# Runs of two, four and eight equal matrix products in the feed-forward stages of a two-layer decoder trunk

## The chip, the cores and the metric

The kernel runs on one core of one Trainium2 chip; the other cores are idle. A core has a matrix engine (TensorE, PE in the profile, with its weight loads shown apart as PEld), a vector engine (DVE), a scalar engine (ACT), a general engine (POOL) and a queue that issues the transfers (SP). The metric is the device time of one execution in microseconds (us); lower is better. The kernel before took 1003.13 us, the median of three runs that lie between 1002.96 and 1003.3 us.

## The reference, cut to what matters

Two layers, each a feed-forward sub-layer, a token-mixing sub-layer and a second feed-forward sub-layer. The input has 256 positions of 1024 features; the feed-forward width is 2816. The change touches the feed-forward sub-layers alone.

```python
def swiglu(h, w_gate_up, w_down):
    a, b = jnp.split(h @ w_gate_up, 2, axis=-1)
    return (jax.nn.silu(a) * b) @ w_down

def hybrid_layer(x, ...):
    x = x + 0.5 * swiglu(rms_norm(x, ffn1_norm), ffn1_w_gate_up, ffn1_w_down)
    ...                                    # pooling and block attention, merged by gates
    x = x + merged @ w_out
    x = x + 0.5 * swiglu(rms_norm(x, ffn2_norm), ffn2_w_gate_up, ffn2_w_down)
    return x
```

All of it is float32. With two layers there are four feed-forward stages, which are called the first to the fourth here, in the order of the program.

## The kernel before

**Numbers.** A float32 matrix is written as the sum of two parts, a high one and a low one, each of a shorter float format that TensorE multiplies quickly. A 128x128 block of weights thus has a high and a low part (`hl[h][:, 0]` and `hl[h][:, 1]`), and so has a 128x256 block of activations (`xk[:, 0]`, `xk[:, 1]`, next to each other). Three of the four partial products are formed, in two instructions. The high weights stay in the array while 512 columns stream past, both parts of the activations; then the low weights, while 256 columns stream past, the high activations alone. These two products together are called a **chain** here (`chain`, L119 to L122). Every product goes through `prod` (L117), which loads its own weights. So PE sees a long sequence of 512, 256, 512, 256, with a weight load ahead of each.

**Tiles.** Weights come in units of 1 MB, each 16 blocks (`unit`, `bring`, L72 to L95): one transfer, then a copy on ACT (high part, L102) and a subtraction on DVE (low part, L103), for each half of 8 blocks. Two units are asked for ahead.

**A feed-forward stage** (`ffn`, L262). In its first part, 22 units are multiplied with the 8 activation blocks `hk`. `pair` (L130 to L138) takes one unit: 8 steps along the features, and in each step one chain for the gate half and one for the up half, which add up in two banks of one PSUM tile (`ps[:, 0]`, `ps[:, 1]`); then ACT (L174) and DVE (L175) drain the tile. The first two units of a stage (three in the first stage) go through `two_pairs` or `pairs`, which have loops of their own. The third unit also carries two small products (`spread`, tile `st`) that sum up squares over the partitions for the norm; they stand ahead of the chain whose number is `at`. Each pair of outputs then becomes a silu, a product and another split on ACT and DVE (L302, L303, L178, L179), into the tiles `ga` (the first 16 blocks) and `gb` (the last 6).

In its second part ("down"), for each of 8 output blocks `f` there are 22 chains over `ga` and `gb` into one PSUM bank (L306 to L321). The 176 chains use 11 units, so that a unit's end and an output's end don't fall together. In the last output block of the fourth stage, `chain3` takes the place of the chain: three products of 256 columns each, so that the ends can be added up at once.

**Order.** PE's order is the order in which the program issues (`manual_schedule` for PE); ACT, DVE and the transfers are placed by a scheduler.

Of the kernel before, what the change touches and what calls it, by code (L numbers as in the profile page):

```python
# [21 lines left out]
NK = D // P  # L22
DFF = 2816
NF = DFF // P
# [11 lines left out]
C_G1, C_GM, C_G2, C_BG, C_PS, NG = 0, 8, 16, 24, 40, 44  # L36
# [3 lines left out]
def trunk_kernel(ctx: ExitStack, tc: tile.TileContext, x_in, w_in, pw_in, qkn_in, rope_in, mask_in, band_in, out):  # L40
    nc = tc.nc
# [30 lines left out]
    def unit():  # L72

        ask(2)
        return ahead.pop(0)

    def ask(n):
        while len(ahead) < n and n_unit[0] < L * LAYER:
            ahead.append(bring(n_unit[0]))
            n_unit[0] += 1  # L80
# [24 lines left out]
    def blk(hl, b, j, n=1):  # L105
        c = b * P % HALF
        return hl[b * P // HALF][:, j, c:c + n * P]


    def steps(z):  # L110

        if len(z.shape) == 3:
            z = z.rearrange("p a s -> p (a s)")
        return z.rearrange("p (s a c) -> p a s c", a=4, c=4)

    def prod(ps, w, xk, first, last):
        return mm(steps(ps), lhsT=w, rhs=steps(xk), start=first, stop=last)  # L117

    def chain(ps, hl, b, xk, first, last):  # L119

        prod(ps, blk(hl, b, 0), xk, first, False)
        return prod(ps[:, 0, :], blk(hl, b, 1), xk[:, 0, :], False, last)  # L122

    def chain3(ps, hl, b, xs, first=True, last=True):
        for i, xk in enumerate(xs):
            prod(ps, blk(hl, b + i, 0), xk[:, 0, :], first and i == 0, False)
            prod(ps, blk(hl, b + i, 0), xk[:, 1, :], False, False)
            prod(ps, blk(hl, b + i, 1), xk[:, 0, :], False, last and i == len(xs) - 1)

    def pair(hl, t, at=None, do=None):  # L130

        ps = pmm.tile([P, 2, 2, S], F32, name="ps", tag="mm")
        for k in range(NK):
            for j in range(2):
                if 2 * k + j == at:
                    do()
                chain(ps[:, j], hl, 2 * k + j, hk[k], k == 0, k == NK - 1)
        return drain(t, ps)  # L138

    def ends():  # L140
# [32 lines left out]
    def drain(t, ps):  # L173
        a = act(t, ps[:, :, 1, :], AF.Copy)  # L174
        return a.ins, tt(t, ps[:, :, 0, :], t, op=OP.add).ins  # L175

    def halves(d, v):
        act(d[:, 0, :], v, AF.Copy)  # L178
        tt(d[:, 1, :], v, d[:, 0, :].bitcast(F32), op=OP.subtract)  # L179
# [4 lines left out]
    x = gx[:, L * NG:].rearrange("p (k s) -> p k s", s=S)  # L184
# [17 lines left out]
    hk = [hx[:, k] for k in range(NK)]  # L202
    acc = acts.tile([P, S], F32, name="acc")

    def split_x(f, l, col):
        g = gain[:, l, col + f:col + f + 1]
        act(hx[:, f, 0, :], x[:, f, :], AF.Copy, scale=g)  # L207
        stt(hx[:, f, 1, :], x[:, f, :], g, hx[:, f, 0, :].bitcast(F32), op0=OP.mult, op1=OP.subtract)  # L208

    def square_x(f):  # L210
        if f == 0:
            act(acc, x[:, f, :], AF.Square)
        else:
            sq = small.tile([P, S], F32, name="sq", tag="sq", bufs=2)
            act(sq, x[:, f, :], AF.Square)
            tt(acc, acc, sq, op=OP.add)

    def prep(f, l, col):
        split_x(f, l, col)
        square_x(f)  # L220
# [13 lines left out]
    def sums():  # L234

        ah = small.tile([P, 2, S], F32R, name="ah", tag="dr", bufs=1)
        halves(ah, acc)
        return ah

    def spread(ah, st):  # L240
        for j in range(2):
            prod(st, one_r, ah[:, j, :], j == 0, j == 1)

    def factor(st):
        r = small.tile([P, S], F32, name="r", tag="r", bufs=2)
        rsqrt(r, st, 1.0 / D)
        return r
# [10 lines left out]
    def bc2(a):  # L258
        return a.unsqueeze(1).to_broadcast([P, 2, a.shape[-1]])


    def ffn(after, at, ah=None, last=False, mid=None):  # L262
        first = ah is not None

        gs = []
        for n, m in (("ga", 16), ("gb", NF - 16)):
            g = acts.tile([P, m, 2, S], F32R, name=n, tag=n)
            gs.extend(g[:, i] for i in range(m))
        n0 = 3 if first else 2
        abs_ = []  # L270
        r = None
        for i in range(NF):
            ab = tmp.tile([P, 2, S], F32, name="ab", tag="t512", bufs=5)
            abs_.append((i, ab))
            if i < n0:
                if i == n0 - 1:
                    (pairs if first else two_pairs)([unit() for _ in abs_], [t for _, t in abs_])
                continue
            if r is None:
                st = pat.tile([P, S], F32, name="st", tag="at")  # L280
                pair(unit(), ab, at, lambda: spread(ah if first else sums(), st))
                if first:
                    ask(2)
                    with tc.issue_after(last_split[1]):
                        r = factor(st)
                else:
                    r = factor(st)
                if not last:
                    rh = small.tile([P, S], F32, name="rh", tag="rh", bufs=1)
                    act(rh, r, AF.Copy, scale=0.5)  # L290
            elif first and i == 9:

                pair(unit(), ab, NK, lambda: spread(ah, pat.tile([P, S], F32, name="st", tag="at")))
            else:
                pair(unit(), ab)
            for j, ab in abs_:
                if last:
                    tt(ab, ab, bc2(r), op=OP.mult)
                else:
                    tt(ab[:, 0, :], ab[:, 0, :], r, op=OP.mult)  # L300
                sg = small.tile([P, S], F32, name="sg", tag="sg", bufs=2)
                act(sg, ab[:, 0, :], AF.Silu)  # L302
                tt(sg, sg, ab[:, 1, :], op=OP.mult)  # L303
                halves(gs[j], sg)
            abs_ = []
        for b in range(NK * NF):  # L306
            f, k = divmod(b, NF)
            if b % 16 == 0:
                hl = unit()
            if mid and b == 32:  # L310
                mid()
            if k == 0:
                ps = pat.tile([P, 2, S], F32, name="ps", tag="at")
            two = not last or f < NK - 1
            if two:
                chain(ps, hl, b % 16, gs[k], k == 0, k == NF - 1)
            else:
                chain3(ps[:, 0, :], hl, b % 16, gs[k:k + 1], k == 0, k == NF - 1)
            if k == NF - 1:
                add_x(f, ps, 0.5, two, None if last else rh)  # L320
                after(f)  # L321

    def add_x(f, ps, c, two=True, rc=None):

        t = x[:, f, :]
        if two:
            t = small.tile([P, S], F32, name="t", tag="sg", bufs=2)
            act(t, ps[:, 1, :], AF.Copy)  # L328
        if rc is not None:
            tt(t, ps[:, 0, :], t, op=OP.add)  # L330
            tt(t, t, rc, op=OP.mult)
            tt(x[:, f, :], x[:, f, :], t, op=OP.add)
            return
        if two:
            stt(t, t, c, x[:, f, :], op0=OP.mult, op1=OP.add)
        stt(x[:, f, :], ps[:, 0, :], c, t, op0=OP.mult, op1=OP.add)  # L336
# [52 lines left out]
    def turns(l):  # L389

        if l == 0:
            with tc.issue_after(last_load[0]):
                for d, z in ((rope, rope_in), (qkn, qkn_in), (mask[:, 1], mask_in), (mask[:, 2], mask_in)):
                    nc.sync.dma_start(d, z)
        cs = []
        for j in range(2):
            c = small.tile([P, 2, 2, DH], F32, name="c", tag="turn", bufs=2)
            with tc.issue_after(last_split[1]):
                for i in range(2):
                    tt(c[:, i], rope[:, i], bc2(qkn[:, l, j, i * DH:(i + 1) * DH]), op=OP.mult)  # L400
            cs.append(c)
        return cs
# [240 lines left out]
    with tc.manual_schedule(engines={E.SP, E.Activation, E.DVE}):  # L643
# [22 lines left out]
        ah = sums()  # L666
# [3 lines left out]
    ahead.extend(w[1] for w in w3)  # L670
    for l in range(L):
        cs = []
        ffn(lambda f: prep(f, l, C_GM), NK if l else NK + 1, None if l else ah, mid=lambda: cs.extend(turns(l)))
        mix(l, lambda f: prep(f, l, C_G2), cs)
        if l + 1 < L:
            ffn(lambda f: prep(f, l + 1, C_G1), NK + 1)
        else:
            ffn(lambda f: nc.sync.dma_start(out[:, f, :], x[:, f, :]), NK + 1, last=True)


# [88 lines left out]
```

## Time and profile before

| what | before |
|---|---|
| device time, median of three runs | 1003.13 us |
| device time of the profiled execution | 1006.28 us |
| its span, from the first to the last instruction | 1004.4 us |
| PE busy in the span | 997.9 us (99%), 6170 products |
| DVE busy | 806.1 us (80%) |
| ACT busy | 636.8 us (63%) |
| mean granted TensorE clock | 0.999 |
| memory traffic over the span | 191 GB/s |

The span is divided into the work of the engines. "Busy" of PE counts the time in which at least one product is under way; products overlap, the next one starting while the one before still drains, so that a busy PE is not the same as a PE at its peak. The chain of waits is the sequence of work, followed back from the last instruction, that set the end. In it, the time of a piece with a count of products divided by that count is the real step from one product to the next.

### The profile page before, as it was taken

The page shows a single profiled execution, that of the slowest core. Times are in us where ns is not written, and L with a number is a line of the kernel's source. Part 1 is how long each engine was busy: PE and PEld are TensorE (multiplying, and loading weights), DVE is VectorE, ACT ScalarE, POOL GpSimd, SP SyncE. Part 2 cuts the span into 40 slices and gives each one's busy share as a digit, 9 for nine tenths or more (in the row PEclk, how much of TensorE's full clock was granted, in tenths as well). Part 3 has the DMA queues.
Part 4 walks back from the last instruction along what each step waited for, and adds up shares of the span by engine and source line. Part 5 has one row for each costly group of instructions (what it writes and reads, how often), then busy time and mean ns, then how long its engine had stood idle before and what let it go on. Part 6 is the DMA issues. An engine that isn't in the chain of part 4 may idle for free.

```text
span 1004.4 us, 15755 instructions
## 1 busy us (share of the span) xinstructions
PE 997.9 (99%) x6170; PEld 898.7 (89%) x6170; DVE 806.1 (80%) x1326; ACT 636.8 (63%) x1017; POOL 10.6 (1%) x35
## 2 busy tenths in 40 slices
PE   9999999999999999999999999999999999999998
PEld 8889899888899988989989899898888989899887
DVE  7887777799978987776778777778997899988752
ACT  7766655657776676665557666556676777666541
POOL 0000000002000000000000000000010000000000
PEclk9999999999999999999999999999999999999999
DMA  8765665553545655655656555554536456555640
GB/s 294 266 230 182 224 210 194 184 199 107 210 168 174 215 205 204 209 184 199 207 173 208 206 201 186 201 209 151 196 119 222 163 195 213 200 191 208 211 146 22
DMA packets 30601, 192.94 MB, mean 192 GB/s; under 512 B 3392, under 2 KB 5824, under 8 KB 8000
## 3 DMA queue, kind: packets, MB, share of 16 engines
q1 hardware_dynamic: 30240, 191.69, 55.4%
q8 instruction: 48, 0.79, 0.3%
q10 hardware_dynamic: 288, 0.26, 0.1%
q14 instruction: 25, 0.20, 0.1%
HBM read 190.89 MB, written 1.05 MB: 191 GB/s over the span
## 4 chain that ended last, share of the span: by engine, by line
PE 97%; DVE 1%; ACT 0%; DMA 0%; issue 0%; SPq 0%
PE ps L117 78%; PE pt L117 9%; PE pl L117 6%; PE pe L117 2%; PE sc L431 1%; DVE hl L103 1%; PE y L467 1%; PE pt L457 1%; PE tp L422 0%; DMA raw<-w 0%; PE yp L117 0%; ACT hl L102 0%; DVE ab L300 0%; DVE r L226 0%; PE st L117 0%
## 5 line engine op out<-in xcount | busy, mean ns | idle before, releaser
L117 PE MATMUL ps<-hx,hl 128*128 128x512 f32 (+1 forms) x3200 | 543.0, 329 | 2.0 <-ACT sg L302 1.4
L117 PEld LDWEIGHTS ps<-hx,hl 128*128 128x128 f32 x3200 | 481.7, 188 | 57.6 <-ACT sg L302 1.7
L103 DVE TENSOR_TENSOR hl<-raw,hl 128x1024 fp32r<-128x1024 f32 (+2 forms) x371 | 439.8, 1192 | 111.7 <-ACT hl L102 110.0
L102 ACT ACTIVATE hl<-raw 128x1024 fp32r<-128x1024 f32 (+2 forms) x371 | 382.7, 1034 | 144.5 <-PE ps L117 98.8
L117 PE MATMUL ps<-ga,hl 128*128 128x256 f32 (+1 forms) x1040 | 176.0, 325 | 0.0
L117 PEld LDWEIGHTS ps<-ga,hl 128*128 128x128 f32 x1040 | 154.3, 188 | 16.6
L174 ACT ACTIVATE ab<-ps 128x512 f32<-128x512 f32 x84 | 50.0, 595 | 80.4 <-PE ps L117 80.1
L175 DVE TENSOR_TENSOR ab<-ps,ab 128x512 f32<-128x512 f32 x84 | 57.7, 687 | 36.5 <-ACT ab L174 36.3
L117 PE MATMUL ps<-gb,hl 128*128 128x256 f32 (+1 forms) x390 | 69.2, 325 | 0.0
L117 PEld LDWEIGHTS ps<-gb,hl 128*128 128x128 f32 x390 | 57.9, 188 | 6.2
L302 ACT ACTIVATE sg<-ab 128x256 f32<-128x256 f32 x88 | 36.2, 417 | 26.7 <-DVE ab L300 15.4
L117 PE MATMUL pt<-ax,hl 128*128 128x256 f32 x384 | 44.5, 276 | 0.0
L117 PEld LDWEIGHTS pt<-ax,hl 128*128 128x128 f32 x384 | 44.2, 188 | 0.3 <-DVE gates L175 0.3
L117 PE MATMUL pl<-hl,hx 128*128 128x512 f32 (+1 forms) x256 | 44.4, 330 | 0.0
L117 PEld LDWEIGHTS pl<-hl,hx 128*128 128x128 f32 x256 | 38.5, 188 | 4.9
L303 DVE TENSOR_TENSOR sg<-sg,ab 128x256 f32<-128x256 f32 x88 | 36.1, 418 | 0.1
L328 ACT ACTIVATE t<-ps 128x256 f32<-128x256 f32 x39 | 14.7, 378 | 27.7 <-PE ps L117 27.7
L178 ACT ACTIVATE ga<-sg 128x256 fp32r<-128x256 f32 x64 | 25.4, 406 | 8.7 <-DVE sg L303 8.5
L207 ACT ACTIVATE hx<-gx 128x256 fp32r<-128x256 f32 x48 | 23.9, 504 | 10.8 <-DVE gx L336 5.2
L300 DVE TENSOR_TENSOR ab<-ab,r 128x256 f32<-128x256 f32 x66 | 27.3, 424 | 1.7
L179 DVE TENSOR_TENSOR ga<-sg,ga 128x256 fp32r<-128x256 f32 x64 | 26.2, 418 | 1.4 <-ACT ga L178 1.4
L208 DVE SCALAR_TENSOR_TENSOR hx<-gx,hx 128x256 fp32r<-128x256 f32 x48 | 22.7, 478 | 3.4 <-ACT hx L207 3.4
(125 smaller groups left out, 685.5 us busy)
## 6 DMA issues: line engine op xcount, KB each, us to landing
raw<-w SPq DMA_DIRECT2D x176, 1024.0 KB, 4.9
raw<-w SPq DMA_DIRECT2D x9, 256.0 KB, 5.7
raw<-w SPq DMA_DIRECT2D x2, 512.0 KB, 6.6
out_dram<-gx SPq DMA_DIRECT2D x8, 128.0 KB, 1.9
gx<-x SPq DMA_DIRECT2D x3, 256.0 KB, 5.4
raw<-w SPq DMA_DIRECT2D x4, 128.0 KB, 4.0
raw<-pw SPq DMA_DIRECT2D x2, 256.0 KB, 2.6
raw<-w ACTq DMA_DIRECT2D x2, 128.0 KB, 3.7
```

Of the source, the lines that this page charges most:

```text
L102: a = act(hi, w, AF.Copy)
L103: last_split[:] = [a.ins, tt(lo, w, hi.bitcast(F32), op=OP.subtract).ins]
L117: return mm(steps(ps), lhsT=w, rhs=steps(xk), start=first, stop=last)
L174: a = act(t, ps[:, :, 1, :], AF.Copy)
L175: return a.ins, tt(t, ps[:, :, 0, :], t, op=OP.add).ins
L178: act(d[:, 0, :], v, AF.Copy)
L179: tt(d[:, 1, :], v, d[:, 0, :].bitcast(F32), op=OP.subtract)
L207: act(hx[:, f, 0, :], x[:, f, :], AF.Copy, scale=g)
L208: stt(hx[:, f, 1, :], x[:, f, :], g, hx[:, f, 0, :].bitcast(F32), op0=OP.mult, op1=OP.subtract)
L300: tt(ab[:, 0, :], ab[:, 0, :], r, op=OP.mult)
L302: act(sg, ab[:, 0, :], AF.Silu)
L303: tt(sg, sg, ab[:, 1, :], op=OP.mult)
```

## The change

The chains of a feed-forward stage are issued in runs. A run of n chains issues first the n products of 512 columns, then the n of 256 columns. In the first stage n is 1, which is the order of before; in the second it is 2, in the third 4, in the fourth 8. Nothing else is computed, and the number of products and of weight loads stays.

```diff
-    def pair(hl, t, at=None, do=None):
+    def run(steps):
+
+        for ps, hl, b, xk, first, last in steps:
+            prod(ps, blk(hl, b, 0), xk, first, False)
+        for ps, hl, b, xk, first, last in steps:
+            prod(ps[:, 0, :], blk(hl, b, 1), xk[:, 0, :], False, last)
+
+    def pair(hl, t, at=None, do=None, n=1):
 
         ps = pmm.tile([P, 2, 2, S], F32, name="ps", tag="mm")
-        for k in range(NK):
-            for j in range(2):
-                if 2 * k + j == at:
-                    do()
-                chain(ps[:, j], hl, 2 * k + j, hk[k], k == 0, k == NK - 1)
+        for b in range(0, 2 * NK, n):
+            if at is not None and b <= at < b + n:
+                do()
+            run([(ps[:, c % 2], hl, c, hk[c // 2], c < 2, c >= 2 * NK - 2) for c in range(b, b + n)])
         return drain(t, ps)
...
+        todo = []
         for b in range(NK * NF):
...
             if two:
-                chain(ps, hl, b % 16, gs[k], k == 0, k == NF - 1)
+                todo.append((ps, hl, b % 16, gs[k], k == 0, k == NF - 1))
+                if len(todo) == group or k == NF - 1 or b % 16 == 15:
+                    run(todo)
+                    todo = []
...
-        ffn(lambda f: prep(f, l, C_GM), NK if l else NK + 1, None if l else ah, mid=lambda: cs.extend(turns(l)))
+        ffn(lambda f: prep(f, l, C_GM), NK if l else NK + 1, None if l else ah, mid=lambda: cs.extend(turns(l)),
+            group=4 if l else 1)
         mix(l, lambda f: prep(f, l, C_G2), cs)
         if l + 1 < L:
-            ffn(lambda f: prep(f, l + 1, C_G1), NK + 1)
+            ffn(lambda f: prep(f, l + 1, C_G1), NK + 1, group=2)
         else:
-            ffn(lambda f: nc.sync.dma_start(out[:, f, :], x[:, f, :]), NK + 1, last=True)
+            ffn(lambda f: nc.sync.dma_start(out[:, f, :], x[:, f, :]), NK + 1, last=True, group=8)
```

`pair` gets `n=group` from `ffn`; `two_pairs`, `pairs`, `chain3` and the whole mixing stage keep their order.

On PE, in the third unit of the second feed-forward stage, this is how the order stood before around the two products of `spread` (tile `st`). A shape 128x4x32x4 is a product of 512 columns, 128x4x16x4 one of 256; the numbers tell buffers apart, `hl_3445` and `hl_3446` being the two halves of one unit.

```order
L117 MATMUL ps_3535<-hx_105,hl_3445 128x4x32x4
L117 MATMUL ps_3535<-hx_105,hl_3445 128x4x16x4
L117 MATMUL ps_3535<-hx_105,hl_3445 128x4x32x4
L117 MATMUL ps_3535<-hx_105,hl_3445 128x4x16x4
L117 MATMUL ps_3535<-hx_105,hl_3446 128x4x32x4
L117 MATMUL ps_3535<-hx_105,hl_3446 128x4x16x4
L117 MATMUL st_3526<-ah_3554,one_r_85 128x4x16x4 x2
L117 MATMUL ps_3535<-hx_105,hl_3446 128x4x32x4
L117 MATMUL ps_3535<-hx_105,hl_3446 128x4x16x4
```

And on PE at the same place of the changed kernel:

```order
L117 MATMUL ps_3535<-hx_105,hl_3445 128x4x32x4 x2
L117 MATMUL ps_3535<-hx_105,hl_3445 128x4x16x4 x2
L117 MATMUL st_3526<-ah_3552,one_r_85 128x4x16x4 x2
L117 MATMUL ps_3535<-hx_105,hl_3446 128x4x32x4 x2
L117 MATMUL ps_3535<-hx_105,hl_3446 128x4x16x4 x2
```

Equal products now stand two and two, and the `spread` stands one chain earlier, ahead of the first block of the second half instead of its second.

On PE, where the fourth stage goes over from its first part to its second, before (the last chain of the last unit, then the first chains of "down"):

```order
L117 MATMUL ps_9375<-hx_105,hl_9319 128x4x32x4
L117 MATMUL ps_9375<-hx_105,hl_9319 128x4x16x4
L117 MATMUL ps_9424<-ga_8296,hl_9368 128x4x32x4
L117 MATMUL ps_9424<-ga_8296,hl_9368 128x4x16x4
L117 MATMUL ps_9424<-ga_8296,hl_9368 128x4x32x4
```

The same place of the changed kernel, on PE, to the start of the second output block (`ps_9482`):

```order
L117 MATMUL ps_9375<-hx_105,hl_9319 128x4x32x4 x8
L117 MATMUL ps_9375<-hx_105,hl_9319 128x4x16x4 x8
L117 MATMUL ps_9424<-ga_8296,hl_9368 128x4x32x4 x8
L117 MATMUL ps_9424<-ga_8296,hl_9368 128x4x16x4 x8
L117 MATMUL ps_9424<-ga_8296,hl_9369 128x4x32x4 x8
L117 MATMUL ps_9424<-ga_8296,hl_9369 128x4x16x4 x8
L117 MATMUL ps_9424<-gb_8297,hl_9417 128x4x32x4 x6
L117 MATMUL ps_9424<-gb_8297,hl_9417 128x4x16x4 x6
L117 MATMUL ps_9482<-ga_8296,hl_9417 128x4x32x4 x2
```

The runs are of eight, but end with a unit or an output block, so that there are also runs of six, four and two in "down". The order on ACT, DVE, POOL and SP is the same row for row as before. Over the whole program, 1025 places where a 256-column product stood behind a 512-column one now have a 512-column product there, and as many have a 256-column product behind a 256-column one: 248 of each in the second stage, 368 in the third, 409 in the fourth.

More of the change, by code (lines that the diff above doesn't have):

```diff
@@ L259, in bc2, with ffn @@
         return a.unsqueeze(1).to_broadcast([P, 2, a.shape[-1]])
-    def ffn(after, at, ah=None, last=False, mid=None):
+    def ffn(after, at, ah=None, last=False, mid=None, group=1):
         first = ah is not None
@@ L280, in ffn @@
                 st = pat.tile([P, S], F32, name="st", tag="at")
-                pair(unit(), ab, at, lambda: spread(ah if first else sums(), st))
+                pair(unit(), ab, at, lambda: spread(ah if first else sums(), st), group)
                 if first:
@@ L294, in ffn @@
             else:
-                pair(unit(), ab)
+                pair(unit(), ab, n=group)
             for j, ab in abs_:
```

## The prediction

> **What bounds the kernel.** I read the page's head first, then the chain of waits.
>
> ```profile
> span 1004.4 us, 15755 instructions
> PE 997.9 (99%) x6170; PEld 898.7 (89%) x6170; DVE 806.1 (80%) x1326; ACT 636.8 (63%) x1017; POOL 10.6 (1%) x35
> PEclk9999999999999999999999999999999999999999
> PE 97%; DVE 1%; ACT 0%; DMA 0%; issue 0%; SPq 0%
> ```
>
> PE is busy throughout, at the full granted clock in every slice, and 97% of the chain that set the end is PE. No other engine can be made to matter without first holding PE up. So the question is one of PE's own pace: the step from one product to the next. A busy share can't show that, since products overlap. The pieces of the chain of waits in order of time do: each has a length and a count.
>
> ```profile
> 342.84 162.37 PE ps L117 x974
> 518.77 162.70 PE ps L117 x976
> 838.39 162.61 PE ps L117 x996
> ```
>
> These are the second, third and fourth feed-forward stage, each from its `spread` to its end, without a gap. The first has 974 products, 487 chains: 162.37 / 487 = 0.3334 us, so **a chain takes 333.4 ns**. The second gives 162.70 / 488 = 333.4 ns again. Inside a chain I look at two narrow windows of the timeline on PE, which show what was running then and when it began.
>
> ```profile
> 400.27 0.49 PE L117 MATMUL ps<-hx,hl 128*128 128x256 f32 x2
> 400.38 0.38 PE L117 MATMUL ps<-hx,hl 128*128 128x512 f32 x1
> 400.38 0.50 PE L117 MATMUL ps<-hx,hl 128*128 128x512 f32 x2
> 400.05 0.49 PE L117 MATMUL ps<-hx,hl 128*128 128x512 f32 x2
> ```
>
> A 512-column product begins at 400.05, its 256-column partner at 400.27, the next 512 at 400.38. To the two digits shown, the 512 holds PE for 0.22 us and the 256 for 0.11 us: 333.4 in all, about 221 and 112.
>
> **What the change removes and adds.** Nothing is removed or added. 1025 times (248, 368 and 409 in stages two to four), a pair of steps "512 then 256, 256 then 512" is exchanged for "512 then 512, 256 then 256". So each exchange costs X + Y - 333.4 ns, where X is the step of a 512 that is followed by a 512, Y that of a 256 followed by a 256.
>
> Y is in the trace. The last output block of the fourth stage is made of `chain3`, 256-column products alone, with the same operands and a weight load for each.
>
> ```profile
> 993.26 5.67 PE L117 MATMUL ps<-ga,hl 128*128 128x256 f32 x48
> 998.77 2.22 PE L117 MATMUL ps<-gb,hl 128*128 128x256 f32 x18
> 780.88 22.20 PE pt L117 x192
> ```
>
> From 993.26 to 998.77 there are 48 of them: 5.51 / 48 = **Y = 114.8 ns**. The branch products of the mixing stage give 22.20 / 192 = 115.6. A check: the fourth stage's piece has 996 products, 66 of them in `chain3`; 465 x 333.4 + 66 x 114.8 ns = 162.6 us, the 162.61 of the row. So a 256 costs some 3 ns more behind its own kind than in a chain, and no more: runs of 256 columns don't run into the weight load, though a load lasts longer than the step:
>
> ```profile
> L117 PEld LDWEIGHTS ps<-hx,hl 128*128 128x128 f32 x3200 | 481.7, 188 | 57.6 <-ACT sg L302 1.7 <-ACT hl L102 0.9 <-DVE hl L103 0.2
> L117 PE MATMUL ps<-ga,hl 128*128 128x512 f32 x496 | 166.8, 382 | 0.0
> L117 PE MATMUL ps<-ga,hl 128*128 128x256 f32 x544 | 141.3, 274 | 0.0
> ```
>
> At 188 ns a load outlasts a 256's step of 114.8, so loads must overlap one another. Were they serial, the exchange would cost 1025 x (188 - 115) ns = 75 us; the 114.8 excludes that.
>
> X is nowhere in the trace: no 512 stands behind a 512. The break-even is X = 333.4 - 114.8 = **218.6 ns**. Bounds from the nearest rows:
>
> - From below: a 512-column product lasts 382 ns, a 256-column one 274, so 256 columns more take 108 ns. 512 columns then take 216 ns with nothing between products. X = 216 would give 1025 x (216 + 114.8 - 333.4) = 1025 x (-2.6) = -2.7 us.
> - From above: Y plus the 108 ns for the further columns, 114.8 + 108 = 222.8, that is 1025 x 4.2 = +4.3 us.
> - In between: the 512's step in a chain, about 221, gives +2.5 us; and if the time of a product depends on its own length and on that of its neighbour, each separately, the sum can't change at all, as every kind of product and of neighbour keeps its count. That is the 218.6.
>
> I take **X = 220**, between the last two, which are the nearest rows: 1025 x (220 + 114.8 - 333.4) = 1025 x 1.4 ns = **+1.4 us**. By stage: +0.35, +0.5 and +0.6.
>
> The Trainium skill, page "TensorE: Matmul & The Clock Gate", section "Back-to-back issue gap", gives the isolated step of a warm product as N/2.4 + 2.5 ns, 215.8 for 512 columns and 109.2 for 256; a chain would be 325.0 by it. The trace's 333.4 and 114.8 are both longer, so it doesn't hold in this stream of loads and products; if it held for the 512s in a run, the sum would be an estimated 1025 x (215.8 + 114.8 - 333.4) = -2.9 us.
>
> **What else moves.** Four edits cost nothing, each with its cover.
>
> ```profile
> 831.82 0.42 DVE L179 TENSOR_TENSOR ah<-acc,ah 128x256 fp32r<-128x256 f32 x1
> 837.99 0.39 PE L117 MATMUL st<-ah,one_r 128*128 128x256 f32 x2
> 941.92 5.49 PE L117 MATMUL ps<-ga,hl 128*128 128x512 f32 x32
> 947.02 0.42 DVE L179 TENSOR_TENSOR gb<-sg,gb 128x256 fp32r<-128x256 f32 x1
> ```
>
> - The `spread` moves one chain earlier, 0.33 us. Its input `ah` is written at 832.24 and it ran at 837.99: 5.4 us of cover remain. Without it, PE would stand, and all behind it.
> - In "down", a run needs its activations earlier. The tightest is the last block of `gb` in the fourth stage, written at 947.44. Before, its 512 began 21 chains into the stretch at 941.92 + 7.00 = 948.92; now it stands behind 16 chains and five 512s, at 941.92 + 5.33 + 1.10 = 948.35. 0.9 us of cover remain; if it were gone, PE would stand by what is missing, once, well under 1 us.
> - The last product into a PSUM tile and the last use of a half unit fall at the ends of runs, where they stood before: runs end at each output block and each unit, and 2, 4 and 8 all divide a half unit of 8 blocks in the first part. In "down", runs that don't start on a multiple of their length free a half up to 8 products later, under 2 us; the next splits go to other buffers, and PE shows no wait for a split in these stages (the pieces above are unbroken).
> - ACT, DVE, POOL and SP keep their order, and the transfers their triggers; DVE and ACT are 20% and 37% idle.
>
> A second weighing: the same page's section "Step-by-step: what each phase is for" says that loads are pulled ahead into a background buffer while a product runs, which speaks against runs of 256, as each load has only a short product to hide under. The 114.8 already holds what that costs here; by the page alone, with the 107 ns a load takes in its section "LDWEIGHTS (loading the stationary operand)", it would be an estimated 109 or so and the sum would fall by 6 us.
>
> **The rivals.**
>
> *A: slower, the rhythm is lost.* The trace has the same chains at other paces, at the same clock.
>
> ```profile
> 703.43 10.85 PE pl L117 x64
> 714.28 10.74 PE pt L117 x64
> 761.65 11.11 PE ps L117 x64
> 813.82 10.67 PE ps L117 x64
> ```
>
> 32 chains each: 339.1, 335.6, 347.2 and 333.4 ns. The third is `pair` itself, with the operands of a feed-forward stage, behind other small products (its start may hold another wait, so I don't price by it). So what a chain costs above its columns, 3 x 108 = 324, depends on how products and loads fall on one another, and 333.4 is the best that any stretch shows. Runs change that rhythm in every chain of three stages: 496 + 496 + 474 = 1466. At the 339.1 of the query and key products it costs 1466 x 5.7 = +8.4 us; at X = 222.8 without more, +4.3. It decides from X + Y over 335.4, where the loss passes 2 us. For it: a 256 behind a 256 already pays 3 ns more. Against it: the feed-forward stages hold their pace over 488 chains, whatever went before. Time: 1005.6 to 1011.5.
>
> *B: faster, switching is what costs.* A chain has 9 ns above its columns, and if most of it comes from the change of length, runs save it. Then X falls to its lower bound, 216, and the time by 2.7 us, to 1000.4. For it: nothing shows a 512 behind a 512, and a longer product hides a load best. Against it: a 256 behind a 256, with no change of length, is not cheaper but dearer.
>
> *C: no change at all,* as the counts of kinds are kept: 1003.1, inside the forecast's band. That the order isn't what it says is excluded: on PE the equal products stand in runs.
>
> **How the numbers follow.** The sum is made against the profiled execution: 1006.28 us of device time, its span of 1004.4 and 1.9 around it. 1006.28 + 1.4 is 0.14% more. The median shown is 1003.13, so the forecast is 1003.13 x 1.0014 = **1004.5 us**. A measurement here can tell about 0.2%, 2 us, from no change; in X that is 216.6 to 220.6 when Y holds. The forecast and C, inside 2 us: 0.40. A: 0.34, as the bound from above and the spread of rhythms both lie there, but the forecast's X is itself only 0.6 ns short of it. B: 0.26. The range has B's 1000.4 in it with a little of a Y below 114.8, and A's price at 339.1 lies above its middle: 999.8 to 1009.5, which leaves out the greater losses (a tenth) and the greater gains (a little less).
>
> **What would show it.** The three pieces of the chain of waits for stages two to four, 162.37, 162.70 and 162.61 us before, should read about 162.7, 163.2 and 163.2. If they fall instead, by an amount that goes with 248, 368 and 409, B is right and X is 218.6 less the fall per exchange. If they rise by 2 us and more, A is right, and the starts in a narrow window tell whether the 512s or the 256s pay. The first stage and the mixing stages must stay as they were; if they move, it is something other than the order. A gap ahead of `st` or in the first output block of "down" would show that a cover was misjudged. The forecast is wrong if X lies outside 216.6 to 220.6.

## The result, and the profile after

The changed kernel takes 1016.54 us (median of four runs, 1016.31 to 1018.21), the kernel before 1003.21 us beside it. The ratio is 1.0128, with a 95% interval from 1.0116 to 1.0141: slower by 13.3 us, outside the predicted range.

The head of the page of the changed kernel, with the same lines as shown of before:

```profile
span 1014.7 us, 15755 instructions
PE 1009.7 (100%) x6170; PEld 901.2 (89%) x6170; DVE 806.1 (79%) x1326; ACT 636.1 (63%) x1017; POOL 10.6 (1%) x35
PEclk9999999999999999999999999999999999999999
PE 99%; DMA 1%; ACT 0%; DVE 0%; issue 0%
```

Nothing waits that did not wait before: the instructions, DVE's and ACT's busy time and the clock are the same, and PE is busy for 11.8 us more. Its busy time grew with the same 6170 products, so the products follow each other more slowly. The chain of waits in order of time shows where; the pieces are the four feed-forward stages (start, length, products):

```profile
58.09 125.33 PE ps L117 x752
340.04 165.91 PE ps L117 x976
519.82 167.99 PE ps L117 x976
844.16 167.07 PE ps L117 x998
```

The first stage, with runs of one, has 376 chains in 125.33 us: 333.3 ns a chain, as before. The second has 165.91 / 488 = 340.0, the third 167.99 / 488 = 344.2, the fourth (167.07 - 66 x 0.1148) / 466 = 342.3, with its 66 `chain3` products taken off. Over 333.4 that is 3.2, 5.3 and 4.1 us, 12.6 of the 13.3. Each exchange of steps cost about 13, 14 and 10 ns, where +1.4 was forecast. (The span grew by 10.3 us only, because the first stage began 2.7 us later in the execution of before that was profiled, whose device time, too, lay 3 us above its median.)

A narrow view shows the products themselves. Groups by shape on PE, from 860 to 930 us, inside the fourth stage; behind the bar stand the time in which the group was at work and the mean length of one product in ns. First before, then after:

```profile
L117 PE MATMUL ps<-hx,hl 128*128 128x512 f32 x211 | 70.4, 382 | 0.0
L117 PE MATMUL ps<-hx,hl 128*128 128x256 f32 x211 | 57.7, 273 | 0.0
```

```profile
L117 PE MATMUL ps<-hx,hl 128*128 128x512 f32 x205 | 51.2, 389 | 0.0
L117 PE MATMUL ps<-hx,hl 128*128 128x256 f32 x206 | 27.7, 276 | 0.0
```

The record of a product is longer, 389 for 382 ns with 512 columns and 276 for 273 with 256. This does not tell a stall within a product from a wait between two: the ends of products are modelled in the profile, and a 512 of the first part is recorded as ending some 160 ns after the next product starts, before (382 and a step of 221) as after (389 and 229). So the starts are used here. From them, the steps that stood open in the prediction are X = 229.1 ns (mean of 680 in the first parts; 226.7 in the 345 of the second parts; 228.3 over all 1025) and Y = 114.7 ns in the first parts, 114.8 over all. In runs of eight of the first parts, the first 512 behind a run of 256s takes 221.6, the second 224.9, the others 228 to 234.

### The profile page after: what moved, and what is told of

Same layout as the page of the kernel before. It is cut to its first block, busy times and chain, and to the rows that moved or that the text cites. A ratio compares the mean times of both kernels' runs of the same rounds, so it can differ in the third digit from the quotient of the medians.

```text
span 1014.7 us, 15755 instructions
## 1 busy us (share of the span) xinstructions
PE 1009.7 (100%) x6170; PEld 901.2 (89%) x6170; DVE 806.1 (79%) x1326; ACT 636.1 (63%) x1017; POOL 10.6 (1%) x35
## 4 chain that ended last, share of the span: by engine, by line
PE 99%; DMA 1%; ACT 0%; DVE 0%; issue 0%
PE ps L117 79%; PE pt L117 9%; PE pl L117 6%; PE pe L117 2%; DMA raw<-w 1%; PE sc L441 1%; PE y L477 1%; PE pt L467 1%; PE tp L432 0%; PE yp L117 0%; PE st L117 0%; ACT L654 0%; DVE hl L103 0%; ACT hl L102 0%; DVE gx L346 0%
## 5 line engine op out<-in xcount | busy, mean ns | idle before, releaser
L117 PE MATMUL ps<-hx,hl 128*128 128x512 f32 (+1 forms) x3200 | 551.5, 332 | 0.4 <-ACT hl L102 0.2
L117 PE MATMUL ps<-ga,hl 128*128 128x512 f32 (+1 forms) x1040 | 180.2, 328 | 0.0
L117 PEld LDWEIGHTS ps<-ga,hl 128*128 128x128 f32 x1040 | 156.9, 188 | 18.4
L117 PE MATMUL ps<-gb,hl 128*128 128x256 f32 (+1 forms) x390 | 71.7, 328 | 0.0
L117 PEld LDWEIGHTS ps<-gb,hl 128*128 128x128 f32 x390 | 60.0, 188 | 6.8
```

## The experiments

Each experiment is one execution with its profile, at a granted clock of 0.996 to 1.000. They are compared by the pace of a chain: the length of a stage's piece in the chain of waits over its chains. Where nothing that matters was changed, a stage's piece repeats to within 0.1 us between executions (the third stage: 167.99 to 168.07). Where a first and a second part are told apart, the pace comes from the starts of the products.

**Run lengths in other stages.**

```diff
-            group=4 if l else 1)
+            group=2 if l else 8)
...
-            ffn(lambda f: prep(f, l + 1, C_G1), NK + 1, group=2)
+            ffn(lambda f: prep(f, l + 1, C_G1), NK + 1, group=16)
...
-            ..., last=True, group=8)
+            ..., last=True, group=4)
```

> The changed kernel with other run lengths: 8, 16, 2 and 4 in the four stages (in place of 1, 2, 4, 8). Theory 'order': the pace of a chain belongs to the length of the run, wherever it stands: about 342 ns in the first stage (8), 340 in the third (2), 344 in the fourth (4), and 342 to 347 with 16 in the second. Theory 'stage': the pace belongs to the stage (its buffers, what the other engines do in it): 333, 340, 344, 342 as in the changed kernel.

The pieces of the first, third and fourth stage:

```profile
59.81 128.46 PE ps L117 x752
526.36 165.91 PE ps L117 x976
848.62 168.20 PE ps L117 x998
```

128.46 / 376 = 341.6 with runs of 8, 165.91 / 488 = 340.0 with 2, to the hundredth what 2 gave in another stage, and 344.7 with 4. In these stages the pace goes with the run length, not with the stage.

The second stage, with runs of 16, is not one piece:

```profile
341.94 114.08 PE ps L117 x664
457.13 1.23 DVE hl L103
458.36 0.35 DVE gb L185
458.75 53.94 PE ps L117 x315
```

Its first part has 342.4 ns a chain. In its second part PE waits once, about 1 us, for a block of `gb` that stands behind a split of weights on DVE: the cover that the prediction weighed for `gb` is gone here. Behind the wait the pace is 53.94 / 157.5 = 342.5.

**No weight traffic beside the products.**

```diff
     def bring(u):
+        layer, v = divmod(u, LAYER)
+        if NF + NF // 2 <= v < NF + NF // 2 + 24:
+            return load(u)
+        stage = layer, v < NF + NF // 2
+        if stage not in kept:
+            kept[stage] = load(u)
+        return kept[stage]
+
+    def load(u):
         raw, hl = buffers()
```

> The changed kernel, runs of 1, 2, 4, 8, but each feed-forward stage loads and splits only one unit of weights and uses it for all its blocks, so that there are no weight transfers and no splits on ACT and DVE while it runs (the products are formed with the wrong weights). Theory 'traffic': runs meet the transfers and splits in the memory; without these, all four stages come to 333 ns a chain or less. Theory 'order': 333, 340, 344 and 342 stay within 2 ns.

The second to fourth stage of this kernel:

```profile
339.94 165.91 PE ps L128 x976
519.47 168.07 PE ps L128 x976
844.07 167.07 PE ps L128 x998
```

165.91, 168.07 and 167.07 us beside 165.91, 167.99 and 167.07: the transfers and splits of weights have no part in it. What is left is PE and the memory it reads and writes.

**512 columns for both products.**

```diff
-            prod(ps[:, 0, :], blk(hl, b, 1), xk[:, 0, :], False, last)
+            prod(ps, blk(hl, b, 1), xk, False, last)
```

> The changed kernel, but the second product of a chain streams 512 columns too (the low weights also meet the low activations, the fourth partial product). In the first stage the loads still alternate between high and low weights, in the others they come in runs of 2, 4 and 8. Theory 'length': a 512 behind a 512 is what costs, whatever it loads; 2 x 229 = 458 ns for two products in all four stages. Theory 'weights': what costs is to load high weights one after another; 2 x 221 = 442 ns in the first stage, 458 in the others.

The pieces of this kernel:

```profile
70.20 165.44 PE ps L117 x752
408.50 226.10 PE ps L117 x976
649.20 226.09 PE ps L117 x976
1046.70 223.45 PE ps L117 x998
```

165.44 / 376 = 440.0 for two products without runs, 463.3, 463.3 and 463.2 with them. So a 512 behind a 512 can take 220.0 ns, the very value that the prediction chose (a coincidence: the prediction had no such stream to read it from), or 231.7. This spoke for 'weights', which expected 442 and 458, and against a fixed price of the length. The next three runs followed it up.

**The same with run lengths 2, 1, 8, 1.**

> All products of 512 columns as in the run before, but run lengths 2, 1, 8 and 1 in the four stages. Theory 'load address' (or any theory by which the order of the products decides): 463 ns for two products in the first and third stage, 440 in the second and fourth. Theory 'state': the pace is a state that a stage falls into at its start and keeps; it is 440 in the first stage and 463 in the others, or mixed without regard to the run length.

```profile
71.22 174.17 PE ps L117 x752
418.35 219.15 PE ps L117 x974
652.47 226.06 PE ps L117 x976
1051.45 216.82 PE ps L117 x996
```

463.2, 450.0, 463.2 and 450.0: 463 wherever there are runs, but 450, not 440, without them. One and the same order of products has more than one steady pace.

**Loads from one block, and loads that alternate.** In the first kernel every load of a unit comes from its first block, in the second high and low weights change places in every second chain:

```diff
-            prod(ps, blk(hl, b, 0), xk, first, False)
+            prod(ps, blk(hl, 0, 0), xk, first, False)        # the first; likewise the low weights
...
-            prod(ps, blk(hl, b, 0), xk, first, False)
+            prod(ps, blk(hl, b, b % 2), xk, first, False)    # the second; 1 - b % 2 for the other
```

> The changed kernel, runs of 1, 2, 4, 8, but every 512-column product of a unit loads the high weights of the unit's first block, every 256-column one the low weights of that block (the products are formed with the wrong weights). Theory 'length': a 512 behind a 512 costs more whatever is loaded: 333, 340, 344 and 342 ns a chain stay. Theory 'load address': the cost of runs comes from loads that follow each other in memory (512 bytes apart); loads from one and the same place change the paces of stages two to four by more than 2 ns.

> The changed kernel, runs of 1, 2, 4, 8, but in every second chain high and low weights change places, so that the loads of a run alternate between the two halves of the weight tile, 4 KB apart, as they do without runs (the products are formed with the wrong weights). Theory 'load address': in the all-512 kernel 220.0 ns a product came with alternating loads and 231.7 with loads in order; so here X = 220, and the paces of stages two to four fall to 333.3 + (220 + 114.8 - 333.3) = 335 or below, the first stage (whose loads still alternate) staying at 333. Theory 'length': 340, 344 and 342 stay.

The second to fourth stage of the second of them:

```profile
342.75 165.91 PE ps L117 x976
522.53 167.99 PE ps L117 x976
846.89 167.07 PE ps L117 x998
```

They are those of the changed kernel to the hundredth, and the first kernel's (165.92, 168.07, 167.07) nearly so. Which block is loaded plays no part in runs; the reading of the all-512 run as 'weights' fell. Only the first stage moved a little, to 336.7 with alternating blocks. In both kernels, though, a load still begins at a multiple of 512 bytes from the start of its tile; the later runs come back to that.

**All products stream block 0.**

```diff
-            prod(ps, blk(hl, b, 0), xk, first, False)
+            prod(ps, blk(hl, b, 0), hk[0], first, False)
```

> The changed kernel, runs of 1, 2, 4, 8, but all products of the runs stream the same activations, block 0 (the products are formed with the wrong activations). Theory 'moving address': the cost of runs comes from where consecutive products read their columns; the paces of stages two to four change by more than 2 ns, and those of a stage's first part (blocks in pairs) and second part become one. Theories 'length' and 'load address': 333, 340, 344 and 342 stay.

The first parts have 333.3, 340.0, 345.5 and 343.2, as in the changed kernel (333.3, 340.0, 345.7 and 343.1). The second parts of three stages can't be used, as block 0 is rewritten while they run and PE waits for it; that of the fourth has 340.6, again as in the changed kernel. So which block streams plays no part either.

**Plain column order.**

```diff
-            prod(ps, blk(hl, b, 0), xk, first, False)
+            mm(ps, lhsT=blk(hl, b, 0), rhs=xk, start=first, stop=False)
```

> The changed kernel, runs of 1, 2, 4, 8, but the products of the runs stream their columns in plain order, from the first to the last, in place of the stepped order (4 columns, then 12 left out, in four sweeps). Theory 'order': stages two to four stay slower than the first, by 6 to 11 ns a chain. Theory 'column order': what runs cost comes from the stepped order, and all four stages come out at one pace.

The starts of the products give 350, 353, 353 and 353. Runs cost 3 ns here and 7 to 11 in the stepped order: both theories are half right. What the stepped order saves, 17 ns a chain, it saves for the alternation above all. The next two runs take the two sides apart.

**Stepped on one side only.** `flat` leaves a block in plain order; the first kernel writes plain, the second reads plain.

```diff
-        return mm(steps(ps), lhsT=w, rhs=steps(xk), start=first, stop=last)
+        return mm(flat(ps), lhsT=w, rhs=steps(xk), start=first, stop=last)     # e9
+        return mm(steps(ps), lhsT=w, rhs=flat(xk), start=first, stop=last)     # e10
```

> The changed kernel, runs of 1, 2, 4, 8, with the stepped column order kept for reading the activations, and plain order for writing the results, in every product of the program (columns land in the wrong places). With plain order on both sides the stages took 350, 353, 353 and 353 ns a chain, with stepped order on both 333, 340, 344 and 342. Theory 'reading': what products lose above their columns, and what runs add, is decided where the activations are read; paces of 333, 340, 344, 342. Theory 'writing': it is decided where results are added up in PSUM; 350, 353, 353, 353.

> The changed kernel, runs of 1, 2, 4, 8, with plain order for reading the activations and stepped order for writing the results, in every product (columns land in the wrong places). Theory 'reading': 350, 353, 353, 353 ns a chain. Theory 'writing': 333, 340, 344, 342. If both this and the run before are slow, the two sides must step alike.

Stages one, two and four of the kernel that reads stepped and writes plain, then of the one that reads plain:

```profile
58.56 125.33 PE ps L120 x752
340.30 165.91 PE ps L120 x976
844.43 167.07 PE ps L120 x998
```

```profile
59.77 131.60 PE ps L120 x752
353.46 172.43 PE ps L120 x976
874.66 172.59 PE ps L120 x998
```

The first are the times of the changed kernel to the hundredth. The second give 131.60 / 376 = 350.0, 172.43 / 488 = 353.3 and, by the starts, 353.3 again (the `chain3` products are slower here, too). It is the order in which the activations are read that decides, both on the pace and on what runs add to it; stepped or plain writing into PSUM makes no difference.

**Other steps, without runs and with runs of eight.**

```diff
-        return z.rearrange("p (s a c) -> p a s c", a=4, c=4)
+        return z.rearrange("p (s a c) -> p a s c", a=how[0][0], c=how[0][1])
```

> The order of before (no runs), with another stepped order in each feed-forward stage: 2 sweeps of groups of 4 columns, 8 sweeps of 4, 4 sweeps of 8, and 4 sweeps of 2, where the kernel has 4 sweeps of 4. Theory 'fit': 333 ns a chain comes from how this stepped order and the alternation of 512 and 256 fall on one another; the four paces differ by several ns, and a better one may be among them (below 333). Theory 'fixed price': a chain costs 333 whatever the steps are, and only plain order is worse.

> The same four stepped orders, with runs of 8 in all stages. Theory 'fit': the extra that runs cost (342 - 333 = 9 ns a chain at 4 sweeps of 4, 3 ns in plain order) differs with the stepped order, and can be nothing or a gain for one of them. Theory 'length': runs cost 7 to 11 ns a chain with every stepped order.

| sweeps x columns in a group | no runs, ns a chain | runs of 8 |
|---|---|---|
| 4 x 4 (the kernel) | 333 | 342 |
| 2 x 4 | 350 | 350 |
| 8 x 4 | 358 | 369 to 370 |
| 4 x 8 | 343 | 345 to 347 |
| 4 x 2 | 693 | 694 |

With other steps runs cost nothing, 2 to 3, or 12 ns: 'fit'. None is a gain, and none beats 333.

**Other ways to load, without runs and with runs of eight.** `far` takes the 128 columns of a load with a stride of 2, 4 or 8 elements, or moved by 4 elements (16 bytes; the last of eight blocks moves back, the others on):

```diff
-            prod(ps, blk(hl, b, 0), xk, first, False)
+            prod(ps, far(hl, b, 0), xk, first, False)
...
+        if n == 0:
+            c = b * P % HALF + (4 if b % 8 < 7 else -4)
+            return hl[b * P // HALF][:, j, c:c + P]
+        c = b % 8 // n * n * P
+        w = hl[b * P // HALF][:, j, c:c + n * P].rearrange("p (c s) -> p s c", s=n)
+        return w[:, b % n, :]
```

> The order of before (no runs) in the feed-forward chains, but the loads take their 128 columns from memory in other ways: every 2nd, every 4th, every 8th element in the first three stages, and 128 neighbouring ones, moved by 16 bytes, in the fourth (blocks of weights are mixed, so the products are formed with wrong weights). Theory 'collision': reading the activations stalls on the weight loads beside it; the paces change with the stride by several ns. Theory 'stream alone': the loads have no part in it; 333 ns a chain in all four.

> The same loads with runs of 8 in all stages. Theory 'collision': the paces differ by stage, as in the kernel without runs or more. Theory 'stream alone': 343 in the first part and 340 in the second, as runs of 8 have it with neighbouring columns.

The four stages without runs, then a load in the third of them (mean of one: 340 ns):

```profile
59.63 131.16 PE ps L117 x752
350.48 230.51 PE ps L117 x974
595.92 239.08 PE ps L117 x976
1011.22 167.11 PE ps L117 x996
```

```profile
L117 PEld LDWEIGHTS ps<-hx,hl 128*128 128x128 f32 x247 | 60.6, 340 | 0.0
```

348.8, 473.3, 489.9 and 343.1 ns a chain. At strides of 4 and 8 the load itself becomes long, 328 and 340 ns for 188, and those two stages may simply wait for it. The fourth stage is the clean one: each load reads as many neighbouring elements as before, 16 bytes away, and still lasts 188 ns, and a chain takes 343.1 for 333.3. With runs of eight the same move goes the other way:

```profile
1009.30 166.26 PE ps L117 x998
```

(166.26 - 7.58) / 466 = 340.5, for 342.3 without the move. 'Stream alone' is out: the pace depends on where the loads beside the products read, though the loads themselves are no longer.

**Moving the activations instead.**

```diff
-    hx = acts.tile([P, NK, 2, S], F32R, name="hx")
+    hx = acts.tile([P, NK * 2 * S + 4], F32R, name="hx")[:, 4:].rearrange("p (k a s) -> p k a s", k=NK, a=2)
...
-            g = acts.tile([P, m, 2, S], F32R, name=n, tag=n)
+            g = acts.tile([P, m * 2 * S + 8], F32R, name=n, tag=n)[:, 8:].rearrange("p (k a s) -> p k a s", k=m, a=2)
```

> The changed kernel, runs of 1, 2, 4, 8, with the activations of the first part of a stage moved by 16 bytes in memory, those of the second part by 32 bytes, the weights staying (the output is the reference's). Theory 'collision' of a kind that depends on which 16-byte pieces meet: the paces change, differently for the two parts. Otherwise 333, 340, 345 and 343 stay in the first part, 333, 340, 342 and 340 in the second.

```profile
58.79 127.73 PE ps L117 x752
344.19 167.91 PE ps L117 x976
526.00 166.76 PE ps L117 x976
850.35 165.43 PE ps L117 x998
```

339.7, 344.1, 341.7 and 338.7 ns for whole stages. The two parts were not moved as intended: in the built program the activations of the first part (`hx`) lie 16 bytes further on, but `ga` 64 and `gb` 96 bytes, as the longer tiles ahead of them push them on. By the starts of the products, in ns a chain:

| runs of | first part, changed kernel | moved by 16 bytes | second part, changed kernel | moved by 64 and 96 bytes |
|---|---|---|---|---|
| 1 | 333.3 | 340.2 | 333.3 | 339.2 |
| 2 | 340.0 | 344.5 | 340.0 | 343.4 |
| 4 | 345.7 | 341.6 | 341.7 | 342.0 |
| 8 | 343.1 | 336.7 | 340.6 | 342.4 |

In the first parts, 16 bytes cost 7 and 4 to 5 ns without runs and with runs of two, and give 4 and 6 back with runs of four and eight. The second parts only lose. The computation is the same and the result too; only the place in memory differs.

**A search for a better meeting, without runs.** Weights read 32 and 48 bytes further on, then 16 and 32 sweeps of the activations.

> The order of before (no runs). First and second stage: weights read 32 and 48 bytes further on (the products are formed with blocks that overlap their neighbours); third and fourth: the right weights, the activations read in 16 and in 32 sweeps of groups of 4 columns. Theory 'collision': moving the weights by 32 or 48 bytes changes the pace as 16 bytes did (343), by several ns either way, and so do the sweeps; a pace below 333 would be a better kernel. If all four are at 333 or above, the kernel before has the best meeting among those tried.

```profile
59.73 127.04 PE ps L119 x752
343.53 166.33 PE ps L119 x974
526.67 201.71 PE ps L119 x976
887.80 194.40 PE ps L119 x996
```

337.9, 341.5, 413.3 and, by the starts, 400.0 ns (the `chain3` products of the fourth stage are slower here, too). Nothing tried beats 333.3, so there is no version to put against the kernel before.

## Why the prediction was wrong, point by point

**What bounds the kernel: right.** PE's own pace is the whole of it. The pieces of the chain of waits carried the result, and the first stage and the mixing stages stayed as they were.

**The sum of the exchanges: the step that failed.** The term X was mis-sized. The prediction put X at 220, "between the last two, which are the nearest rows", with 222.8 as the bound from above. Measured X is 228.3 over the 1025 exchanges, 229.1 in the first parts and 226.7 in the second. With it the prediction's own sum gives 1025 x (228.3 + 114.8 - 333.4) = +9.9 us, where it had +1.4. The bound added the columns of a longer product to the step of a shorter one, as if what a product loses above its columns were a fixed amount. The runs show that it depends on how the activations are read, and that it grows and shrinks with the order and with the place in memory; the all-512 kernel has 220.0, 225.0 and 231.7 for the same step. The 218.6 of the additive argument fell for the same reason.

**That only the exchanged steps change: also wrong.** The steps from 512 to 256 and from 256 to 512 that remain at the ends of runs take 224.3 and 115.4 ns in the mean, for 221.3 and 112.1 before: 2.8 us more, which the sum did not have. With the 9.9 this is the 12.6 of the pieces to 0.1 us. With runs of two, where such steps are most, they are nearly half of the loss: in the first part of the second stage, one exchange adds up as 512 to 512 226.4 (+7.8 over 218.6), 512 to 256 224.2 (+2.9 over 221.3), 256 to 256 114.2 (-0.6 under 114.8) and 256 to 512 115.1 (+3.0 over 112.1), 13.1 ns together.

**The sign** came out as forecast, but by luck: +1.4 us lay within the 2 us that the prediction itself counted as no change, and its X was a value between two bounds of which neither held what happened.

**Y: right.** 114.8 was taken from `chain3`, and 114.8 was measured in the runs. Though a load is recorded with 188 ns, a run of 256s is not slowed to it.

**What else moves: right.** With runs up to eight, `spread`, `gb` and the buffers cost nothing; the stages' pieces are unbroken, and the kernel without weight transfers and splits has the same paces. With runs of 16 the cover of `gb` was gone, for about 1 us.

**Rival A was the way it went,** with a chance of 0.34. It said that what a chain costs above its columns depends on how products and loads fall on one another; the runs bear that out, and its threshold was passed. Its price was too low. I took the 339.1 ns of the query and key products and set the 347.2 of `pair` in the mixing stage aside, because a wait might lie in it; so the upper end of the range lay 7 us short. The starts in the trace of before show how long that wait is: the first step takes 333 ns where the later steps of a 512 take 220 to 231, about 0.11 us of the 11.11. Behind it the steps repeat every four chains, 110, 221, 118, 226, 109, 231, 121 and 231 ns. That is a steady 341.8 ns a chain, without runs and with the operands of a feed-forward stage. Priced by it, A would have been 1466 x 8.4 = +12.3 us, where +13.3 was measured; no run explains why the paces with runs (340.0, 344.2 and 342.3) lie so near to it. The same stretch answers the argument against A, that the feed-forward stages hold their pace "whatever went before": one order can hold more than one steady pace, 333.4 and 341.8 here, 440 and 450 in the all-512 kernels. That 333.4 was "the best that any stretch shows" should have weighed more.

**Rival B** and the Trainium skill's isolated step of 215.8 ns ("TensorE: Matmul & The Clock Gate", "Back-to-back issue gap"): no stream with loads reached it; the shortest steady 512 was 220.0. The same page's "Step-by-step: what each phase is for" gives TensorE two read ports of its own, so that loading the next weights takes nothing from the running product. The traces don't bear that out for this stream: loads that read 16 bytes away, each as long as before, moved a chain from 333.3 to 343.1 ns.

**Shown and not shown.** Shown: the loss depends on the column order in which the activations are read, on how the 256s and 512s follow each other, and on the place in memory of the loads and of the activations, to 16 bytes. The transfers and splits of weights, plain or stepped writing into PSUM and the choice of block have no part in what runs add. Not shown: that the two reads collide in the memory is the reading that fits, but no run shows the collision itself, nor that it is the place of the one relative to the other that counts, as no run moved both alike. Open: by what rule a rhythm settles, why the same order has 440 in one stage and 450 in others (and 333.4 and 341.8 in the kernel before), and why runs of four are the worst.

## What to carry to other kernels

Where an engine streams back to back, treat the step measured in one order as a property of that order, column pattern and placement. Before reordering, look for the same products at other paces in the trace; when the present pace is the best of them, as it was here, a reordering has more to lose than to win. A row that may hold a wait can still be priced: the starts within it tell the wait from the pace. A sum that moves parts between neighbours needs the step itself measured, which one stage of one run would have given.

## What the runs showed of the hardware that was not expected

- Moving the activations of a first part by 16 bytes in memory, with the same products and loads, changed a chain by -6 to +7 ns of 340.
- Reading activations in groups of 2 columns (8 bytes) doubled the time: 693 ns a chain for 333 with groups of 4, though the count of columns is the same.
- A weight load of every eighth element took 340 ns for 188, and chains took 490 ns.
- One order of equal products can hold several steady paces: 220.0, 225.0 or 231.7 ns for a 512 behind a 512, the first two of them in the same order.
- The times of a stage repeat to the hundredth of a microsecond between kernels that differ in transfers, in PSUM order or in the blocks they read: 165.91 us with runs of two in five of them.
